# Out-projection by Strassen's seven products, with sums made beside the mixer, and the sums of w_ff1 on GpSimd in the first third of ff1

## The chip, the cores and the metric

The kernel runs on one core of one Trainium2 chip. The metric is the device time of one execution in microseconds. A core has five engines that run their own streams of instructions and wait for each other by semaphores: TensorE (PE, with its weight loads, PEld), VectorE (DVE), ScalarE (ACT), GpSimd (POOL) and SyncE (SP). In this kernel SP issues every DMA.

## What is computed

One layer of a streaming encoder. 2048 prompt rows and 128 rows of running streams make 17 chunks of 128 tokens; the model is 1024 wide. Cut to what matters here:

```python
proj = einsum('bld,de->ble', x, w_in)                  # in-projection
y_g = gmlp(proj)      # u * (W_s v + b), v normalised   (1024 wide)
y_s = ssd(proj)       # Mamba-2 scan, gated norm        (1024 wide)
h = einsum('ble,ed->bld', concatenate([y_g, y_s]), w_out)   # out-projection, 2048 -> 1024
x = layer_norm(ALPHA * x + h)
x = layer_norm(ALPHA * x + square(relu(x @ w_ff1)) @ w_ff2)  # 1024 -> 4096 -> 1024
```

## The kernel before

**Precision.** Every large matmul is made of three: both operands are split into a rounded high part and a rest (`split`: ScalarE casts, VectorE subtracts, L54 to L56), and high x high, high x low and low x high are summed in PSUM (`PASSES`).

**The mixer** (`mixer_heads`, L91) runs the in-projection in three blocks of 6, 6 and 5 chunks. A block has 18 units, each with one weight tile of 2 MB (`load_w`, L112) that is loaded one unit ahead into one of two buffers. The results u, v, z and xs go to DRAM. Between units, tasks of a list run, one per unit: `ssd` (chunk by chunk and by two groups) writes its rows to `ys_d`, `gmlp` (L511) reads v and u, makes the gate on TensorE (`sg`, L537), finishes it on VectorE (`og`, L545) and GpSimd (`ug`, L546), and writes `yg_d` (L547). yg is stored with features on the partitions, as the out-projection's matmuls need it, ys with tokens on the partitions; `load_blocks` and `flip` (L34 to L43) turn it in 32 x 32 squares by four DMAs and a VectorE transpose. The gMLP of the last block's five chunks (12 to 16) is left over when the in-projection ends; `mixer_heads` returns `run`, by which out_proj starts these tasks as `tail`.

**The out-projection** (`out_proj`, L617) holds all of w_out in SBUF, split, in eight tiles (`wout`, from loads `wos`). It goes chunk by chunk: 16 feature blocks, three passes and two halves of the output are 96 matmuls of 128x512 (L683). The first group has chunks 0 and 1, 192 matmuls, and `tail(1)` is called before each of its eight weight tiles. For each chunk `load_yg` and `load_ys` load and split the mix (`mx`); after the matmuls VectorE adds the residual (L708) and makes the LayerNorm (`layer_norm`, L604), and the row goes to `x1_d`. While this goes on, `during_out_proj` (L799) makes sums of w_ff1 (`w1_piece`, L771) on VectorE and stores them, and the first sums of x (`x_piece`).

**The FFN** (`ffn`, L815) already works by Strassen's seven products (Winograd's form) in 2 x 2 blocks: chunks are paired as in `THIRDS`, features halved. ff1 goes in thirds of the chunks, each over 16 groups g of w_ff1, loading the plain parts (`w1l`, `w1r`) and the stored sums (`w1s`). In thirds 2 and 3 `w2_piece` (L785) makes the sums of w_ff2 and stores them for ff2, which goes product by product.

**What sets the order.** The tile framework schedules the program ahead of time and fixes a stream for each engine; a tile that takes the place of another waits until that one's last reader is done. SP's stream is in order: a DMA that waits holds all those behind it. The DMAs share eight completion semaphores in turn.

## Time and profile before

| what | us |
|---|---|
| median of 3 runs (2840.2 to 2848.67) | 2842.54 |
| the profiled execution | 2838.33 |
| its span | 2836.5 |
| mixer: up to the first out-projection matmul | 0 to 1066.8 |
| out_proj, TensorE busy 386.49 of 1066 to 1471 | 1066.8 to 1471 |
| ff1, TensorE busy 677.84 of 1479 to 2174 | 1478.9 to 2174 |
| ff2 and the end, TensorE busy 647.91 of 2174 to 2836 | 2174 to 2836.5 |

The profile shows one execution. Section 1 of its page gives busy time by engine. A row of a group of instructions names line, engine, operation and tiles with their count, then busy time and the mean duration in ns, then the idle time of the engine ahead of them with what ended it. A row of a table by windows gives start and end, the length, the busy time of PE, PEld, DVE, ACT and POOL with their instructions, the granted TensorE clock, the DMA engines' busy share and GB/s. A row of the timeline gives start, duration, engine, line, operation and, in brackets, idle time before it with its releaser. A DMA row ends with KB of one and us from issue to landing.

### The profile page before, as it was taken

What the parts mean: (1) busy time and instruction counts of PE and PEld (TensorE: products, weight loads), DVE (VectorE), ACT (ScalarE), POOL (GpSimd) and SP (SyncE); (2) the same over time, 40 slices, a digit from 0 to 9 for tenths busy, and PEclk for the clock granted to TensorE, in tenths of its full rate; (3) what the DMA queues carried; (4) which work ended last, traced back from release to release, by engine and by line L of the source; (5) the groups of instructions that cost most, each with busy time, mean ns of one, the idle gap of its engine ahead of it and who ended that gap; (6) DMA issues with size and microseconds to landing.
All of it is one profiled execution on the core that took longest, in us unless ns stands there. A gap on an engine that the chain in (4) does not pass through costs nothing.

```text
span 2836.5 us, 42155 instructions
## 1 busy us (share of the span) xinstructions
PE 2755.8 (97%) x15814; PEld 2525.9 (89%) x15814; DVE 1811.7 (64%) x2852; ACT 1097.7 (39%) x2024; POOL 395.0 (14%) x547
## 2 busy tenths in 40 slices
...
GB/s 316 255 301 247 280 295 258 226 224 212 225 299 228 253 204 306 274 262 264 160 225 356 325 341 354 348 305 241 280 235 237 159 163 187 172 149 180 257 216 167
DMA packets 490012, 708.21 MB, mean 250 GB/s; under 512 B 74304, under 2 KB 378832, under 8 KB 483280
## 3 DMA queue, kind: packets, MB, share of 16 engines
...
HBM read 474.04 MB, written 231.39 MB: 249 GB/s over the span
## 4 chain that ended last, share of the span: by engine, by line
PE 76%; DMA 12%; DVE 7%; SPq 1%; issue 1%; ACT 1%; POOL 1%; ACTq 0%; DVEq 0%; POOLq 0%
PE pf L880 22%; PE pf L1068 21%; PE psfl L231 12%; PE pstl L239 10%; PE po L683 4%; PE yd L446 2%; DMA w1s<-w1p 2%; DMA w1p<-in_w_ff 2%; PE pf L1033 2%; DMA xv<-xtt 1%; PE sg L537 1%; PE st L483 1%; DMA e<-at 1%; DMA v<-vo 1%; PE yo L489 1%
## 5 line engine op out<-in xcount | busy, mean ns | idle before, releaser
L880 PE MATMUL pf<-xt,w 128*128 128x384 f32 (+1 forms) x4032 | 672.9, 329 | 24.7 <-ACT w L55 13.6
L880 PEld LDWEIGHTS pf<-xt,w 128*128 128x128 f32 x4032 | 669.5, 189 | 28.2 <-ACT w L55 14.4
L1068 PE MATMUL pf<-w,ht 128*128 128x512 f32 x2688 | 618.0, 389 | 0.7 <-ACT ht L55 0.7
L1068 PEld LDWEIGHTS pf<-w,ht 128*128 128x128 f32 x2688 | 504.4, 188 | 105.8 <-ACT ht L55 1.1
L231 PE MATMUL psfl<-xw,w 128*128 128x384 f32 (+1 forms) x2880 | 495.5, 330 | 0.1
L231 PEld LDWEIGHTS psfl<-xw,w 128*128 128x128 f32 x2880 | 475.9, 188 | 9.4 <-issue 9.0
L239 PE MATMUL pstl<-w,xw 128*128 128x256 f32 (+1 forms) x3264 | 410.2, 286 | 8.5 <-ACT w L55 6.6
L239 PEld LDWEIGHTS pstl<-w,xw 128*128 128x128 f32 x3264 | 395.6, 189 | 21.3 <-issue 12.0
L683 PE MATMUL po<-wout,mx 128*128 128x512 f32 x1632 | 378.9, 393 | 14.1 <-ACT mx L55 9.7
L683 PEld LDWEIGHTS po<-wout,mx 128*128 128x128 f32 x1632 | 308.2, 190 | 81.4 <-ACT mx L55 10.7
L56 DVE TENSOR_TENSOR ht<-hr,ht 128x1536 fp32r<-128x1536 f32 (+1 forms) x84 | 132.3, 1576 | 185.2 <-ACT ht L55 183.3
L55 ACT CAST ht<-hr 128x1536 fp32r<-128x1536 f32 (+1 forms) x84 | 112.3, 1337 | 214.8 <-PE pf L1068 192.7
L76 POOL TENSOR_SCALAR frs<-fmv 128x1 f32<-128x1 f32 x17 | 8.9, 525 | 1303.0 <-DVE fmv L987 1302.4
L56 DVE TENSOR_TENSOR w<-w2r,w 128x512 fp32r<-128x512 f32 x192 | 124.5, 684 | 61.1 <-ACT w L55 60.9
L55 ACT CAST w<-w2r 128x512 fp32r<-128x512 f32 x192 | 110.9, 618 | 135.5 <-PE pf L1068 93.4
L55 ACT CAST w<-w1s 128x512 fp32r<-128x512 f32 x192 | 118.1, 619 | 83.7 <-PE pf L880 74.3
L56 DVE TENSOR_TENSOR w<-w1s,w 128x512 fp32r<-128x512 f32 x192 | 131.3, 687 | 25.8 <-ACT w L55 19.9
L308 DVE SCALAR_TENSOR_TENSOR acc<-raw,cw,acc 128x640 f32<-128x640 f32 (+1 forms) x108 | 114.0, 1055 | 18.3 <-ACT acc L302 16.9
L438 ACT ACTIVATE e<-e,nacum 128x128 f32<-128x128 f32 x272 | 83.6, 389 | 71.9 <-POOL e L69 71.9
L247 ACT ACTIVATE gt<-gt 128x256 f32<-128x256 f32 (+1 forms) x116 | 52.3, 451 | 95.2 <-DVE gt L246 95.2
L871 ACT ACTIVATE hc<-hc 128x384 f32<-128x384 f32 (+3 forms) x144 | 87.1, 608 | 2.0
L55 ACT CAST mx<-mxs 128x512 fp32r<-128x512 f32 x34 | 20.1, 620 | 171.2 <-PE po L683 87.2
...
## 6 DMA issues: line engine op xcount, KB each, us to landing
...
w<-w_x SPq DMA_DIRECT2D x12, 2048.0 KB, 10.4
w1r<-in_w_ff SPq DMA_DIRECT2D x48, 512.0 KB, 7.9
...
w2r<-w2s SPq DMA_DIRECT2D x80, 256.0 KB, 4.6
ws<-in_w_in SPq DMA_DIRECT2D x34, 512.0 KB, 7.5
e<-at SPq DMA_DIRECT2D x34, 512.0 KB, 7.0
```

The costliest lines, as they stand in the source:

```text
L55: nc.scalar.copy(hi, src)
L56: nc.vector.tensor_sub(lo, src, hi.bitcast(F32))
L231: nc.tensor.matmul(ps[:, :n], w[:, a, k, f * P:(f + 1) * P], xw[:, b, k, o:o + n], start=(q, i, k) == KORDER[0], stop=(q, i, k) == KORDER[-1])
L239: nc.tensor.matmul(ps[:, :n], xw[:, a, k, j * P:(j + 1) * P], w[:, b, k, :n], start=(q, i, k) == KORDER[0], stop=(q, i, k) == KORDER[-1])
L308: nc.vector.scalar_tensor_tensor(aa, raw[:, k:k + npr], cw[:, ft, k:k + 1], aa, op0=ALU.mult, op1=ALU.add)
L438: nc.scalar.activation(e[:, h], e[:, h], AF.Exp, bias=s["nacum"][:, i:i + 1])
L446: nc.tensor.matmul(yd[:, h * HD:(h + 1) * HD], e[:, h], xdt[:, h * HD:(h + 1) * HD], start=True, stop=True)
L683: nc.tensor.matmul(acc[c][d], m[c][k // 4][:, a, k % 4], W[q][:, w, i, d * 512:(d + 1) * 512], start=k == 0 and (a, w) == (0, 0), stop=k = ...
L871: nc.scalar.activation(t, t, AF.Square)
L880: nc.tensor.matmul(o, W[i][:, u, k], X[i][:, v, k, :n], start=q + k == 0 and not more, stop=q == 2 and k == 3, skip_group_check=True)
L1033: nc.tensor.matmul(ps[d], h[:, u, k, f], w[d][:, v], start=k + f + q == 0, stop=(k, f, q) == (n - 1, 1, 2))
L1068: nc.tensor.matmul(acc[l], h[:, u, m, j * P:(j + 1) * P], w[m][:, v], start=kg + q + m == 0, stop=(kg, q, m) == (3, 2, 3))
```

## The change

The out-projection becomes Strassen's as well. Two chunks l and r are the row blocks of a 2 x 2 form, and the 2048 features and 1024 outputs are halved: the first half of the features is half of yg and half of ys. Eight pairs, (0,3), (1,4), (2,5), (6,9), (7,10), (8,11), (12,14) and (13,15), need seven products each, chunk 16 four plain ones (1, 2, 0, 3): 60 products of 24 matmuls of 128x512.

- The task `mix` replaces `gmlp`. After the gMLP of a pair's right chunk it makes the pair's sums: for yg (part 0) four loads of 256 KB, for ys (part 1) 16 loads of 64 KB and four transposes; four sums of 128x512 on VectorE in each part; 11 stores to `mv[p]`. That is 31 DMAs a pair. Sums, loads and the gMLP use one ring of eight tiles (`half`).
- w_out is no longer kept whole: `load_w(i)` loads the parts of one product's weights, subtracts on VectorE, and splits. A product's weights are loaded during the product before. `seq` gives the order: product 1 of all pairs and chunk 16, then 2, 0 (chunk 16 alone), 6, 7, 5, and 4 and 3 alternating.
- The partial results stay in SBUF (`y`, 17 tiles). The residual's additions (`add_x`) are made by GpSimd in product 5, and GpSimd multiplies and adds in the LayerNorm of the left chunks (`finish`); the right ones' is on VectorE.
- `tail(1)` is called ahead of the first five pairs of product 1, and the rest at the sixth.
- The first `x_piece` calls move behind product 3 of pairs 1 to 3.
- `w1_piece` goes. In ff1's first third GpSimd makes the sums of w_ff1, four operations of 128x512 for each g, and stores them; the other thirds load them.
- `w2_piece` goes. ff2's weight loads subtract on VectorE (32 operations of 128x1024), and product 4 runs ahead of 3. The residual there is added in halves between passes.

```diff
+THIRDS = [([0, 1, 2], [3, 4, 5]), ([6, 7, 8], [9, 10, 11]), ([12, 13], [14, 15])]
+ODD = 16
...
+    partner = {r: (k, l) for k, (l, r) in enumerate(p for t in THIRDS for p in zip(*t))}
+
+    def flipped(c, q):
+        s = half("fs").rearrange("p (a f) -> p a f", a=4)
+        for i in range(4):
+            nc.sync.dma_start(s[32 * i:32 * i + 32],
+                              ys_d[c][:, 256 * i + 128 * q:256 * i + 128 * q + 128].rearrange("(a j) f -> j a f", j=32))
+        t = half("ft").rearrange("p (k t) -> p k t", k=4)
+        flip(nc, t, s)
+        return t
+
+    def mix(b, j):
+        gmlp(b, j)
+        r = BLOCKS[b][0] + j
+        if r == ODD:
+            for q in range(2):
+                nc.sync.dma_start(mv[-1][:, 4, 4 * q:4 * q + 4], flipped(r, q))
+        if r not in partner:
+            return
+        p, l = partner[r]
+        for part in range(2):
+            tile4 = lambda name: half(name).rearrange("p (k t) -> p k t", k=4)
+            if part == 0:
+                a11, a12, a21, a22 = (tile4("ma") for i in range(4))
+                for t, c, q in ((a11, l, 0), (a12, l, 1), (a21, r, 0), (a22, r, 1)):
+                    nc.sync.dma_start(t, yg_d[c][:, 4 * q:4 * q + 4])
+            else:
+                a11, a12, a21, a22 = (flipped(c, q) for c in (l, r) for q in range(2))
+                nc.sync.dma_start(mv[p][:, 4, :4], a11)
+                nc.sync.dma_start(mv[p][:, 4, 4:], a12)
+                nc.sync.dma_start(mv[p][:, 5, 4:], a22)
+            to = lambda v: mv[p][:, v, 4 * part:4 * part + 4]
+            s1, s2, s3 = (tile4(f"ms{i}") for i in range(3))
+            nc.vector.tensor_add(s1, a21, a22)
+            nc.sync.dma_start(to(2), s1)
+            nc.vector.tensor_sub(s2, s1, a11)
+            nc.sync.dma_start(to(0), s2)
+            nc.vector.tensor_sub(s3, a11, a21)
+            nc.sync.dma_start(to(1), s3)
+            nc.vector.tensor_sub(s1, a12, s2)
+            nc.sync.dma_start(to(3), s1)
...
-            tasks += [(gmlp, b, j) for j in range(n)]
+            tasks += [(mix, b, j) for j in range(n)]
...
+    yl = pool("yl", 1)
+    wr = pool("owr", 4)
+    mp = pool("mo", 3)
+    mr = pool("mr", 2)
+    wq = pool("wq", 16)
...
+    b11, b12, b21, b22 = ((f, d) for f in range(2) for d in range(2))
+    PARTS = {1: (b11,), 2: (b21,), 3: (b22,), 6: (b11, b12, b22), 7: (b12, b22), 5: (1,), 4: (2, b21), 0: (b12,)}
...
+    def load_w(i):
+        out = []
+        for k in range(4):
+            s = None
+            for n, part in enumerate(PARTS[i]):
+                t = wr.tile([P, 2, 512], F32, name="wor", tag="wr")
+                load_part(t, part, k)
+                if n:
+                    nc.vector.tensor_sub(t, t, s)
+                if n and i == 6:
+                    nc.sync.dma_start(made[k][n - 1], t)
+                s = t
+            for m in range(2):
+                w = wq.tile([P, 2, 512], F32R, name="wo", tag="w")
+                split(w[:, 0], w[:, 1], s[:, m])
+                out.append(w)
+        return out
+
+    V = {6: 0, 7: 1, 5: 2, 3: 3}
+
+    def load_mix(i, p):
+        s = mr.tile([P, KD, P], F32, name="mxs", tag="mr")
+        if p < len(pairs) and i in V:
+            nc.sync.dma_start(s, mv[p][:, V[i]])
+        else:
+
+            c = ODD if p == len(pairs) else pairs[p][i == 4]
+            k = slice(0, 4) if i in (0, 1) else slice(4, 8)
+            nc.sync.dma_start(s[:, :4], yg_d[c][:, k])
+            nc.sync.dma_start(s[:, 4:], mv[p][:, 5 if i == 4 else 4, k])
+        t = mp.tile([P, 2, KD, P], F32R, name="mx", tag="mx")
+        split(t[:, 0], t[:, 1], s)
+        return t
+
...
+    def add_x(c, x, d):
+        h = slice(512 * d, 512 * d + 512)
+        nc.gpsimd.tensor_add(y[c][:, h], y[c][:, h], x[:, h])
...
+        eng.tensor_mul(y[c], y[c], g1)
+        eng.tensor_add(y[c], y[c], b1)
+        nc.sync.dma_start(x1_d[c], y[c])
...
+        if i == 5:
+            nc.vector.tensor_add(yd, yc, ps)
+            nc.vector.tensor_add(yb, yb, ps)
+            x = scaled(l)
+            add_x(l, x, 0)
+            add_x(l, x, 1)
+            x = scaled(r)
+            add_x(r, x, 0)
+            add_x(r, x, 1)
+        if i == 4:
+            stat(r, 1)
+            stat(l, 0)
+            nc.vector.tensor_add(yc, yc, ps)
+            finish(r, (0,), nc.vector)
+        if i == 3:
+            nc.vector.tensor_add(yb, yb, ps)
+            finish(l, (1,), nc.gpsimd)
+
+    n = len(pairs)
+    seq = [(i, p) for i in (1, 2) for p in range(n + 1)] + [(0, n)] + [(i, p) for i in (6, 7, 5) for p in range(n)]
+    seq += [(4, 0)] + [s for p in range(n - 1) for s in ((4, p + 1), (3, p))] + [(3, n - 1), (3, n)]
...
+        nx = order.index(i) + 1
+        if nx < len(order) and order[nx] not in W and (p == 0 or i == 0):
+            W[order[nx]] = load_w(order[nx])
+        if k + 1 < len(seq):
+            ahead[seq[k + 1]] = load_mix(*seq[k + 1])
+        mx = ahead.pop((i, p))
+        at += 1
+        if i == 1 and p < 5:
+            tail(1)
+        acc = pss[at % len(pss)].tile([P, 512], F32, name="po", tag="a")
+        for q, (u, v) in enumerate(PASSES):
+            for m in range(KD):
+                nc.tensor.matmul(acc, mx[:, u, m], W[i][m][:, v], start=q + m == 0, stop=(q, m) == (2, KD - 1))
+        if (i, p) == (1, 5):
             tail(NCH)
             right.close()
...
+            g1 = cp.tile([P, D], F32, name="g1")
+            nc.sync.dma_start(g1, A["ln1_g"].unsqueeze(0).to_broadcast([P, D]))
+            b1 = cp.tile([P, D], F32, name="b1")
+            nc.sync.dma_start(b1, A["ln1_b"].unsqueeze(0).to_broadcast([P, D]))
+        evict(i, p, acc)
+        if i == 3 and 1 <= p <= 3:
+            sums.x_piece(0, p - 1)
...
-    def w1_piece(self, g, ring):
...
-    def w2_piece(self, g):
...
-        w = wr.tile([P, 4, P], F32, name="w1l", tag="wr")
-        nc.sync.dma_start(w, A["w_ff1"][g][:, :4, :P])
+        w = wr.tile([P, 4, 2, P], F32, name="w1l", tag="wr")
+        if b == 0:
+            nc.sync.dma_start(w.rearrange("p k f n -> p k (f n)"), A["w_ff1"][g][:, :4])
+        else:
+            nc.sync.dma_start(w[:, :, 0], A["w_ff1"][g][:, :4, :P])
         v = wr.tile([P, 4, 2, P], F32, name="w1r", tag="wr")
         nc.sync.dma_start(v.rearrange("p k f n -> p k (f n)"), A["w_ff1"][g][:, 4:])
         s = sump.tile([P, 2, 4, 2, P], F32, name="w1s", tag="ws")
-        nc.sync.dma_start(s.rearrange("p h k f n -> p h (k f n)"), sums.w1[g])
-        return {1: w, 2: v[:, :, 0], 4: v[:, :, 1], 6: s[:, 0, :, 0], 7: s[:, 0, :, 1], 3: s[:, 1, :, 0], 5: s[:, 1, :, 1]}
+        flat = s.rearrange("p h k f n -> p h (k f n)")
+        a11, a21, a12, a22 = (t[:, :, f] for t in (w, v) for f in range(2))
+        s2, s3, s4, s1 = (s[:, h, :, f] for h in range(2) for f in range(2))
+        if b == 0:
+            nc.gpsimd.tensor_add(s1, a21, a22)
+            nc.gpsimd.tensor_sub(s2, s1, a11)
+            nc.gpsimd.tensor_sub(s3, a11, a21)
+            nc.gpsimd.tensor_sub(s4, a12, s2)
+            nc.sync.dma_start(sums.w1[g], flat)
+        else:
+            nc.sync.dma_start(flat, sums.w1[g])
...
-        if b > 0 and g % 2:
-            sums.w2_piece(8 * (b - 1) + g // 2)
...
+    t1, t2 = (lambda g: [made[g][0]]), (lambda g: [made[g][1]])
+    PARTS = {1: (b11,), 2: (b21,), 3: (b22,), 6: (b11, b12, b22), 7: (b12, b22), 5: (t1,), 4: (b21, t2)}
...
+                if n:
+                    nc.vector.tensor_sub(t, t, s)
+                    if i == 6:
+                        nc.sync.dma_start(made[g][n - 1], t)
...
-    runs = [(i, (0, 1, 2)) for i in (1, 2, 6, 7, 5, 3)] + [(4, (0, 1)), (4, (2,))]
+    runs = [(i, (0, 1, 2)) for i in (1, 2, 6, 7, 5, 4)] + [(3, (0, 1)), (3, (2,))]```

The order in which the instructions stand shows what becomes of the seam between mixer and out-projection. First SyncE's queue at the mixer's end. The program before: `w_v` is a weight tile of the last units, `v<-vo` are stores of the last units' results, `ys` are SSD rows, `wos` are parts of w_out.

```order
L117 DMA w<-w_v_3834 128x16x256 [waits DMAHW7_49,PE_49]
L631 DMA wos<-in_w_out 128x1024 [waits DMAHW0_49,DVE_49]
L266 DMA v_8147<-vo 128x5x256 [waits DMAHW1_49,DVE_49]
L523 DMA v<-v_8147 128x512 [waits DMAHW3_49,DMAHW2_49,DMAHW1_49]
L525 DMA ug<-u_8146 128x4x128
L631 DMA wos<-in_w_out 128x1024 [waits DMAHW4_49,DMAHW0_49,DVE_49]
L266 DMA v_8147<-vo 128x5x256 [waits DMAHW5_49,DVE_49]
L631 DMA wos<-in_w_out 128x1024 [waits DMAHW6_49,DMAHW4_49,DVE_49]
```

The changed program at the same place: `g` and `b` are ln1's rows, `wor` are parts of product 1's weights, `mxs` is the mix of the first pair.

```order
L839 DMA g_12563<-in_ln_g 128x1024 [waits DMAHW4_49,PE_49]
L511 DMA ys_109<-xs 128x512 [waits DMAHW5_49,DVE_49]
L841 DMA b_12565<-in_ln_b 128x1024 [waits DMAHW6_49]
L269 DMA v_8339<-vo 128x5x256 [waits DMAHW7_49,DVE_49]
L687 DMA wor<-in_w_out 128x2x512 [waits DMAHW3_49]
L687 DMA wor<-in_w_out 128x2x512 [waits DMAHW1_49]
L687 DMA wor<-in_w_out 128x2x512 [waits DMAHW2_49,Activation_49]
L687 DMA wor<-in_w_out 128x2x512
L550 DMA yg_88<-ug 128x512 [waits DMAHW4_49,Pool_49]
L721 DMA mxs<-yg_76 128x512 [waits DMAHW5_49]
L722 DMA mxs<-mv_127 128x512 [waits DMAHW6_49]
```

Before, parts of w_out stand between the last units' stores. Now product 1's weights stand behind g's load, whose semaphore from PE is reached by the last matmul of the in-projection (the tile takes the place of the mixer's `xw`).

Second, TensorE's stream around the leftover gMLPs. The program before: `sg` is half a gMLP, `po` the out-projection.

```order
L537 MATMUL sg<-wt,v 128x128 x4
L683 MATMUL po<-wout,mx 128x512 x79
L537 MATMUL sg<-wt,v 128x128 x4
L683 MATMUL po<-wout,mx 128x512 x5
L537 MATMUL sg<-wt,v 128x128 x4
L683 MATMUL po<-wout,mx 128x512
L537 MATMUL sg<-wt,v 128x128 x4
L683 MATMUL po<-wout,mx 128x512 x11
L537 MATMUL sg<-wt,v 128x128 x8
L683 MATMUL po<-wout,mx 128x512 x24
```

The changed program, from the two halves of chunk 14's gMLP on:

```order
L540 MATMUL sg<-wt,v 128x128 x4
L829 MATMUL po<-wo,mx 128x512 x32
L540 MATMUL sg<-wt,v 128x128 x4
L829 MATMUL po<-wo,mx 128x512 x64
L540 MATMUL sg<-wt,v 128x128 x8
L829 MATMUL po<-wo,mx 128x512 x24
L540 MATMUL sg<-wt,v 128x128 x8
L829 MATMUL po<-wo,mx 128x512 x1272
```

The first x8 is chunk 15's gMLP, the x24 behind it product 1 of the pair 13/15, and the last x8 chunk 16's. Six products of other pairs stand ahead of chunk 15's.

Third, SyncE's queue further on, where chunk 15's v is loaded (`L526`, as `L523` before). The program before, with loads of w_out and of w_ff1's pieces between the gMLPs:

```order
L547 DMA yg_90<-ug 128x512
L631 DMA wos<-in_w_out 128x1024
L547 DMA yg_90<-ug 128x512
L525 DMA ug<-u_8146 128x4x128
L631 DMA wos<-in_w_out 128x1024
L523 DMA v<-v_8147 128x512
L783 DMA w1s_11521<-w1p 128x1024
```

The changed program: `fs` are quarters of the SSD rows of chunks 12 and 14, `ft` their transposes, `ms` sums, `mv_133` the stored mix of the pair 12/14.

```order
L564 DMA fs<-ys_105 32x4x128 x5
L587 DMA mv_133<-ft 128x512
L564 DMA fs<-ys_107 32x4x128 x4
L588 DMA mv_133<-ft 128x512
L722 DMA mxs<-mv_133 128x512
L564 DMA fs<-ys_107 32x4x128 x4
L589 DMA mv_133<-ft 128x512
L593 DMA mv_133<-ms_12255 128x512
L526 DMA v<-v_8339 128x512
L595 DMA mv_133<-ms_12256 128x512
```

The load of chunk 15's v now stands behind the sums of the pair 12/14 and their stores.

262 lines of the change are left out of this document (118 added, 144 removed).

## The prediction

> **What bounds the kernel now.** I read the page's busy shares first, then one table of busy time by windows, then TensorE's timeline around the start of out_proj.
>
> ```profile
> span 2836.5 us, 42155 instructions
> PE 2755.8 (97%) x15814; PEld 2525.9 (89%) x15814; DVE 1811.7 (64%) x2852; ACT 1097.7 (39%) x2024; POOL 395.0 (14%) x547
> L683 PE MATMUL po<-wout,mx 128*128 128x512 f32 x1632 | 378.9, 393 | 14.1 <-ACT mx L55 9.7
> ```
>
> TensorE is busy for 97% of the span, so a matmul that goes is worth its time, provided that nothing new makes TensorE wait. Only some 80 us of the span are TensorE idle; the change must not add to them. The windows' columns are length, then busy time of PE, weight loads, DVE, ACT, POOL, then granted clock, DMA share and GB/s.
>
> ```profile
> 400.00:800.00 400.00, 395.16 (x2713) 382.11 (x2712) 236.46 (x429) 129.69 (x319) 119.82 (x146) 0.99 0.73 236
> 1060.00:1100.00 40.00, 34.44 (x189) 29.20 (x188) 30.91 (x63) 12.08 (x21) 10.82 (x15) 0.96 0.87 275
> 1100.00:1140.00 40.00, 36.22 (x161) 28.93 (x160) 29.91 (x47) 10.34 (x11) 10.00 (x6) 0.92 0.95 324
> 1160.00:1200.00 40.00, 40.00 (x178) 33.12 (x177) 19.50 (x27) 4.98 (x8) 4.20 (x4) 1.00 0.79 244
> 1480.00:1520.00 40.00, 30.61 (x145) 28.50 (x144) 35.28 (x49) 20.88 (x33) 2.87 (x4) 0.84 1.05 380
> 1520.00:1720.00 200.00, 200.00 (x1155) 200.00 (x1154) 152.90 (x267) 111.44 (x194) 0.00 (x0) 1.00 0.98 337
> 2400.00:2836.50 436.50, 421.91 (x1861) 348.69 (x1859) 273.49 (x336) 157.69 (x195) 32.82 (x51) 0.99 0.58 191
> ```
>
> In 1160 to 1200 out_proj alone runs without a gap: 40.00/178 = 0.2247 us a matmul. The seam where the mixer ends (1060 to 1140) costs 5.56 + 3.78 = 9.3 us of TensorE idle, though five chunks of gMLP still run there: the out-projection's first two chunks fill the waits.
>
> ```profile
> 1065.01 1.05 PE L537 MATMUL sg<-wt,v 128*128 128x128 f32 x8
> 1066.82 1.19 PE L683 MATMUL po<-wout,mx 128*128 128x512 f32 x4 [0.76 <-ACT mx L55]
> 1125.74 74.43 PE L683 MATMUL po<-wout,mx 128*128 128x512 f32 x327 [1.55 <-DVE wout L637]
> ```
>
> Out_proj's first matmul stands 0.76 us after the mixer's last; its weights were already in SBUF.
>
> **1. Matmuls.** 17 x 16 x 3 x 2 = 1632 become 60 products of 24 = 1440. 192 x 0.2247 = **-43 us**. (The group's busy time gives 378.9/1632 = 0.232 us, so 45; its mean of 393 ns counts the overlap of neighbours and isn't used.) TensorE bounds this stage, so the saving stands wherever the matmuls run without gaps.
>
> **2. The seam.** This is the largest term. Three things change there. In the new order g1's load waits for the mixer's last matmul, and the queue SP is in order: the weights of product 1 and its first mixes stand behind it. Call that matmul's end T0. Second, products need whole pairs: pairs 12/14 and 13/15 exist only when mix has read both chunks' gMLP and SSD rows back from DRAM, added, and stored. So "with the mixer" holds for six pairs; the sums of the last two are made inside out_proj, on TensorE's path. Third, product 1 has one matmul step per pair (24 x 0.2247 = 5.4 us), not 192 matmuls, to put between two gMLPs.
>
> ```profile
> DMA packets 12462, 20.58 MB, mean 322 GB/s; under 512 B 937, under 2 KB 7252, under 8 KB 12459
> yg<-ug SPq DMA_DIRECT2D x10, 256.0 KB, 6.3
> v<-v SPq DMA_DIRECT2D x9, 256.0 KB, 6.4
> ```
>
> ```profile
> mxs<-yg SPq DMA_DIRECT2D x2, 512.0 KB, 3.4
> mys<-ys SPq DMA_DIRECT2D x8, 128.0 KB, 2.8
> ```
>
> ```profile
> L37 SPq DMA_DIRECT2D mys<-ys x68: 302/427/1153, 1072.0 to 1411.4; - x68
> DMA to landing us min/median/max: 2.0/4.1/10.0
> ```
>
> ```profile
> L546 POOL TENSOR_TENSOR ug<-ug,og x34: 1268/1672/2202, 393.1 to 1124.6; 128x512 f32<-128x512 f32 x34
> DMA to landing us min/median/max: 3.2/5.2/9.1
> ```
>
> ```profile
> L545 DVE SCALAR_TENSOR_TENSOR og<-sg,lgh,cst 128x128 f32<-128x128 f32 x136 | 38.0, 340 | 10.6 <-PE sg L537 10.6
> L778 DVE TENSOR_TENSOR w1p<-w1p 128x512 f32<-128x512 f32 x16 | 11.0, 689 | 60.7 <-DMA w1p<-in_w_ff 55.4 <-issue 5.3
> L43 DVE STREAM_TRANSPOSE myt<-mys 128x1024 f32<-128x1024 f32 x17 | 21.1, 1243 | 16.5 <-DMA mys<-ys 16.3
> L55 ACT CAST mx<-mxs 128x512 fp32r<-128x512 f32 x34 | 20.1, 620 | 171.2 <-PE po L683 87.2 <-DMA mxs<-yg 79.2 <-DVE x L612 4.8
> ```
>
> These are the seam's DMAs (1066 to 1130), the same kinds in a quiet stretch (1375 to 1440), issue and landing of ys and yg, and the arithmetic of a hop.
>
> - Start: g1, b1, one v, four weight parts and the first mix are 4.8 MB; at 322 GB/s, 15 us idle before the first product.
> - Six steps (6 x 5.4) and six half gMLPs (6 x 1.06) then run to T0 + 54, where TensorE comes to chunk 15's gMLP. Its v load stands on SP behind all of mix(12,14). Counted in the new order, 50 DMAs with 17 MB stand from T0 to that mix's last yg load, 12 of them weight parts of 0.5 MB (6.3 MB), among them four of product 6, which are wanted 90 us later: 17/322 = T0 + 53. Then, one after another on SP: landing 3.4; four sums 4 x 0.69 = 2.8; three times four ys loads, a half transpose and the store that waits for it (1.7 + 2.8 + 0.6 = 5.1 each); the load of the stored mix, which waits for that store, 2.0; two sums 1.4; v's landing 3.4. That is 28, so v comes at T0 + 80 and TensorE idles 26.
> - From chunk 15's gMLP to product 1 of pair 13/15: four og 1.4, two GpSimd multiplications 3.3, store 3.4, loads 3.4, sums 2.8, two rounds of ys 10.2, store 2.0, mix load 3.4, cast and subtraction 1.3: 31, of which 30 idle.
> - Chunk 16's rows, with product 1 of 13/15 running beside, 7.
>
> 15 + 26 + 30 + 7 = 78; less the 9 of before, **+69**. With every landing at ys's least, 2.0, and the 380 GB/s of 1480 to 1520, the parts are 13, 15, 23 and 0: +41. With landings at the medians of the busy seam (4.1 to 6.4): 15, 38, 40, 10: +94. I take the quiet stretch's landings, as SP itself waits in most of these hops and so little else flies.
>
> The Trainium skill, DMA: Bandwidth & Descriptors, section "Anatomy of one DMA", gives a DMA about 2.0 us fixed plus its bytes at 436 GB/s, fitted on another issuing path; as an estimate a 256 KB load is then 2.6 us, and the term would be near +46. The trace's yg row, 3.2 at the least, stands above it.
>
> **3. Products 5, 4, 3.** GpSimd now makes the residual's additions (32 of 128x512) and half the LayerNorm's multiplications and additions (16 of 128x1024, each like two).
>
> ```profile
> L76 POOL TENSOR_SCALAR lrs<-lmv 128x1 f32<-128x1 f32 x17 | 16.9, 994 | 330.0 <-DVE lmv L609 330.0
> L77 POOL TENSOR_TENSOR lrs<-lrs,mhalf 128x1 f32<-128x1 f32 x17 | 13.1, 768 | 1.4
> L991 POOL TENSOR_SCALAR fnm<-fmv,frs 128x1 f32<-128x1 f32 x17 | 12.4, 734 | 1.6
> ```
>
> (32 + 32) x 1.67 = 107, and 17 x (0.99 + 0.77 + 0.73) = 42: 149 us of GpSimd against 25 steps x 5.4 = 135 of TensorE, and ff1's first rows wait for the last LayerNorms. **+12**, 0 to 30.
>
> **4. The mixer's blocks.** Each pair adds 31 DMAs, 31 x 0.43 = 13 us of SP, and up to 14 of them stand between two weight loads.
>
> ```profile
> w<-w_u SPq DMA_DIRECT2D x4, 2048.0 KB, 9.0
> ```
>
> A unit lasts 1066/54 = 20 us, the load 9.0 of them, 14 issues 6: about 5 us are left for waits within a mix, and a mix has several. DVE's additional 48 us (8 pairs x 8 sums x 0.69, and half transposes) and 38 MB lie under the matmuls (59% and 73% in 400 to 800). **+8**, 0 to 30.
>
> **5. ff1 and ff2.** 64 GpSimd sums x 1.67 = 107 us within a third of ff1's 695 (1479 to 2174), 232, ahead of splits on DVE, 76% busy (1520 to 1720): **+2**, 0 to 15. ff1's start, 9.4 us idle in 1480 to 1520 before, may win those or lose as many: 0. The w_ff1 pieces' 64 DVE operations in out_proj and their 32 MB were under matmuls: nothing. The w_ff2 sums move from ff1 to ff2, where DVE is 63% busy: nothing; without that cover 32 x 1.25 = 40.
>
> Sum: -43 + 69 + 12 + 8 + 2 = **+48**. The profiled run took 2838.33 us for its span of 2836.5, 0.15% under the median of 2842.54, so I put the sum on the median: **2890 us**. A measurement of this kernel tells about 0.3%, 8.5 us, from no change.
>
> **The rivals.**
> - A, faster: the seam stays covered, since v arrives when TensorE comes for it. For it: five gMLPs cost 9.3 us before with loads of 6.4. Against it: there nothing was read back and added in between. It decides if chunk 15's v lands by T0 + 54. Then -43, with terms 3 to 5 between 0 and 22: 2800 to 2821, say **2811**. Chance 0.18.
> - B, the seam at its lower bound: -43 + 41 + half of 22 = +9, **2851**. For it: in the quiet stretch landings were already at 2.8, near that least. Against it: the seam's own medians are twice as long. 0.14.
> - D, slower: the mixer's weight loads fall behind on SP. From 5 us of waits a mix the next unit starts late; ten boundaries with 6 us more: +60 in place of +8, **2942**. For it: each sum's store waits for DVE on SP. Against: two weight buffers. 0.12.
> - E, slower: GpSimd and DVE take turns.
>
> ```profile
> L501 DVE TENSOR_TENSOR xs<-xs,yt x32: 635/1100/1551, 190.3 to 1027.4; 128x512 f32<-128x512 f32 x32
> L56 DVE TENSOR_TENSOR wout<-wos,wout 128x1024 fp32r<-128x1024 f32 x8 | 9.7, 1220 | 9.7 <-ACT wout L55 9.7
> ```
>
> One addition of the same shape takes 0.64 to 1.55 us in the mixer, where GpSimd works too. If they exclude each other, products 5 to 3 need GpSimd 64 x 1.27 + 42 = 123 and DVE's two-input SBUF operations, 25 mixes and 18 of r's LayerNorm x 1.22 + 16 weights x 0.7 = 64: 187 against 135 is +52, 40 more than term 3: **2930**. 0.10. The Trainium skill, SBUF — State Buffer, section "Who interferes with whom", states such an exclusive lock against GpSimd; L501's spread agrees with it, while a mixer that is 99% TensorE shows it can be harmless.
>
> **How the numbers follow.** The forecast has 0.46, around it the terms' bounds taken as independent give 2858 to 2935. The range 2815 to 2940 takes in B, E, half of A and half of D, and leaves out some 0.15 to 0.2. Faster: A's 0.16 and 0.04 of B, 0.20. Same: 0.02 of A, 0.05 of B, 0.03 of the forecast, 0.10. Slower: the rest, 0.70.
>
> **What would show it.** Right: out_proj's first product starts some 15 us after the mixer's last matmul; TensorE's timeline shows two gaps of over 20 us, before chunk 15's sg (released by DVE's v, behind it SP) and before product 1 of pair 13/15 (by ACT's mx); then steps of 5.4 us without gaps until product 5. Wrong: gaps in product 1 of under 30 us together (A), weight waits at unit boundaries in the mixer above 20 us (D), L501-like rows growing in products 5 to 3 with mx released late (E).

## The result, and the profile after

The changed kernel takes 2953.72 us (2951.94 to 2962.46), the one before 2841.37: 1.0395 of it, 95% interval 1.0366 to 1.0424. It is slower, as forecast, but by 112 us where 48 were forecast, and lies outside the range. The profiled execution has a span of 2952.2 against 2836.5, 115.7 more.

The page's first lines and the groups of the in-projection, the out-projection and ff1:

```profile
span 2952.2 us, 42598 instructions
PE 2746.5 (93%) x15622; PEld 2514.5 (85%) x15622; DVE 1932.6 (65%) x2917; ACT 1199.7 (41%) x2148; POOL 584.2 (20%) x678
...
L968 PE MATMUL pf<-xt,w 128*128 128x384 f32 (+1 forms) x4032 | 678.6, 330 | 45.3 <-ACT xt L57 41.4
...
L234 PE MATMUL psfl<-xw,w 128*128 128x384 f32 (+1 forms) x2880 | 494.4, 331 | 19.7 <-DMA w<-w_u 14.3
...
L829 PE MATMUL po<-wo,mx 128*128 128x512 f32 x1440 | 345.2, 402 | 68.8 <-ACT mx L57 60.6
```

TensorE's idle time is now 206 us (2952.2 - 2746.5) where it was 81 (2836.5 - 2755.8). Most of the difference stands in three places: in the mixer, two thirds of it in front of weights; in front of out_proj's mixes and gMLPs; and in front of ff1's X.

The same division of the span in both kernels by windows: the mixer (two rows), out_proj, the start of ff1, the rest. Before:

```profile
0.00:520.00 520.00, 501.22 (x3296) 477.98 (x3297) 343.86 (x602) 213.83 (x461) 152.35 (x244) 0.99 0.86 277
520.00:1066.80 546.80, 541.95 (x3904) 520.59 (x3902) 324.95 (x559) 186.47 (x484) 161.23 (x204) 1.00 0.72 232
1066.80:1471.40 404.60, 386.79 (x1704) 317.57 (x1704) 243.85 (x353) 56.30 (x82) 45.70 (x44) 0.98 0.78 245
```

After, with out_proj in three rows (seam, middle, products 5 to 3):

```profile
0.00:520.00 520.00, 497.00 (x3243) 474.37 (x3244) 344.06 (x599) 212.99 (x460) 142.81 (x235) 0.98 0.87 279
520.00:1117.40 597.40, 563.40 (x3957) 535.86 (x3955) 352.59 (x628) 185.19 (x483) 170.71 (x213) 0.98 0.80 257
1117.40:1244.30 126.90, 62.05 (x264) 50.86 (x264) 57.70 (x107) 29.29 (x46) 17.61 (x15) 0.72 0.75 250
1244.30:1450.00 205.70, 196.32 (x856) 161.78 (x857) 124.37 (x142) 89.05 (x119) 40.50 (x27) 0.98 0.71 234
1450.00:1562.00 112.00, 96.49 (x394) 76.25 (x392) 97.84 (x110) 37.97 (x39) 67.81 (x61) 0.95 0.69 215
1562.00:1635.00 73.00, 28.95 (x121) 26.80 (x122) 52.64 (x53) 27.92 (x36) 36.17 (x29) 0.67 0.96 317
```

- **Mixer**: 1066.8 to 1117.4, **+50.6**. TensorE idle there 1117.4 - 497.0 - 563.4 = 57.0 against 23.6: +33.4. Of its waits 22.5 are for weight loads that land late (19.7 in the group of L234, 2.8 at L242), where before there was 0.1; those for a gMLP's v rose from 1.0 to 8.4. The other 17.2 are busy time for the same matmuls, beside a lower granted clock (0.98 in these two rows, 0.99 and 1.00 before).
- **Out_proj**: 404.6 to 444.6, **+40.0**. Busy 386.8 to 354.9: -31.9 where 192 matmuls at full clock are -43, so 11 went to slower matmuls (clock 0.72 in the seam). Idle 17.8 to 89.7: +71.9, 64.9 of it in the seam.
- **From out_proj's last matmul to ff1's first**: 7.5 to 32.5, **+25.0**. From there to the end: 1357.6 and 1357.7.

TensorE's timeline of the seam and of ff1's start:

```profile
1116.35 1.05 PE L540 MATMUL sg<-wt,v 128*128 128x128 f32 x8
1136.35 7.15 PE L829 MATMUL po<-wo,mx 128*128 128x512 f32 x24 [18.95 <-ACT mx L57]
...
1160.49 14.79 PE L829 MATMUL po<-wo,mx 128*128 128x512 f32 x64
1193.06 2.08 PE L540 MATMUL sg<-wt,v 128*128 128x128 f32 x8 [17.79 <-DVE v L529]
1196.86 2.08 PE L540 MATMUL sg<-wt,v 128*128 128x128 f32 x8 [1.73 <-DVE v L529]
1222.60 8.29 PE L829 MATMUL po<-wo,mx 128*128 128x512 f32 x24 [23.66 <-ACT mx L57]
```

```profile
1594.52 1.65 PE L968 MATMUL pf<-xt,w 128*128 128x384 f32 x4 [32.53 <-ACT xt L57]
```

What X waits for in those 32.5 us is this:

```profile
1580.51 2.34 POOL L755 TENSOR_TENSOR y<-y,b 128x1024 f32<-128x1024 f32 x1
1582.87 0.33 SPq L756 DMA_DIRECT2D x<-y  x1
1585.55 0.91 SPq L916 DMA_DIRECT2D xr<-xv  x2
```

GpSimd's last LayerNorm addition of a left chunk ends at 1582.85, its row is stored, and X's first load (`xr`) is issued 2.7 us behind that store.

The seam is as foretold: 19 us before the first product, 18 before chunk 15's gate, 24 before product 1 of its pair. What the forecast did not have are the size of the mixer's loss and ff1's start. In the mixer a weight load is late because of what stands ahead of it on SP. Its queue before the 5.9 us wait at 611 to 617:

```profile
599.50 0.34 SPq L587 DMA_DIRECT2D mv<-ft  x1
599.93 0.38 SPq L426 DMA_DIRECT2D bc<-bc  x1
600.37 1.96 SPq L564 DMA_DIRECT2D fs<-ys  x4
602.42 0.38 SPq L588 DMA_DIRECT2D mv<-ft  x1
602.90 0.38 SPq L428 DMA_DIRECT2D e<-at  x1
603.32 1.87 SPq L564 DMA_DIRECT2D fs<-ys  x4
605.23 0.43 SPq L282 DMA_DIRECT2D z<-zo  x1
605.76 0.54 SPq L120 DMA_DIRECT2D w<-w_u  x1
```

Eight loads and two stores of a mix and three other DMAs go ahead of the 2 MB of `w<-w_u` in these 6 us, and each store waits for a transpose. The unit whose buffer these weights take had ended at 594.5, so the load goes out 11 us late; the weights then need 11 us more.

### The profile page after: what moved, and what is told of

Read it like the earlier page. It is cut to its first block, busy times and chain, and to the rows that moved or that the text cites. A ratio compares the mean times of both kernels' runs of the same rounds, so it can differ in the third digit from the quotient of the medians.

```text
span 2952.2 us, 42598 instructions
## 1 busy us (share of the span) xinstructions
PE 2746.5 (93%) x15622; PEld 2514.5 (85%) x15622; DVE 1932.6 (65%) x2917; ACT 1199.7 (41%) x2148; POOL 584.2 (20%) x678
## 4 chain that ended last, share of the span: by engine, by line
PE 65%; DMA 15%; DVE 8%; POOL 3%; SPq 3%; issue 3%; ACT 2%; DVEq 0%; ACTq 0%; POOLq 0%
PE pf L1185 21%; PE pf L968 19%; PE psfl L234 9%; PE pstl L242 7%; PE po L829 4%; PE yd L449 2%; DMA xts<-x 2%; PE pf L1150 1%; DMA wor<-in_w_out 1%; DMA e<-at 1%; DMA fs<-ys 1%; DMA w<-w_z 1%; DMA mv<-ms 1%; SPq L564 1%; DMA v<-v 1%
## 5 line engine op out<-in xcount | busy, mean ns | idle before, releaser
L968 PE MATMUL pf<-xt,w 128*128 128x384 f32 (+1 forms) x4032 | 678.6, 330 | 45.3 <-ACT xt L57 41.4
L968 PEld LDWEIGHTS pf<-xt,w 128*128 128x128 f32 x4032 | 675.0, 189 | 49.0 <-ACT xt L57 43.5
L234 PE MATMUL psfl<-xw,w 128*128 128x384 f32 (+1 forms) x2880 | 494.4, 331 | 19.7 <-DMA w<-w_u 14.3
L234 PEld LDWEIGHTS psfl<-xw,w 128*128 128x128 f32 x2880 | 479.6, 190 | 24.0 <-issue 23.5
L242 PE MATMUL pstl<-w,xw 128*128 128x256 f32 (+1 forms) x3264 | 412.6, 286 | 12.0 <-ACT w L57 6.8
L242 PEld LDWEIGHTS pstl<-w,xw 128*128 128x128 f32 x3264 | 399.2, 191 | 21.8 <-issue 8.7
L829 PE MATMUL po<-wo,mx 128*128 128x512 f32 x1440 | 345.2, 402 | 68.8 <-ACT mx L57 60.6
L829 PEld LDWEIGHTS po<-wo,mx 128*128 128x128 f32 x1440 | 278.6, 195 | 133.2 <-ACT mx L57 63.7
L58 DVE TENSOR_TENSOR ht<-hr,ht 128x1536 fp32r<-128x1536 f32 (+1 forms) x84 | 132.3, 1578 | 128.0 <-ACT ht L57 125.9
L57 ACT CAST ht<-hr 128x1536 fp32r<-128x1536 f32 (+1 forms) x84 | 112.2, 1337 | 194.4 <-PE pf L1185 152.5
L58 DVE TENSOR_TENSOR w<-w1s,w 128x512 fp32r<-128x512 f32 x192 | 143.0, 748 | 34.2 <-ACT w L57 30.6
L57 ACT CAST w<-w1s 128x512 fp32r<-128x512 f32 x192 | 117.9, 616 | 51.5 <-PE pf L968 41.5
L57 ACT CAST w<-w2r 128x512 fp32r<-128x512 f32 x144 | 83.1, 618 | 86.9 <-PE pf L1185 57.8
L58 DVE TENSOR_TENSOR w<-w2r,w 128x512 fp32r<-128x512 f32 x144 | 93.8, 687 | 35.3 <-ACT w L57 34.8
L57 ACT CAST mx<-mxs 128x1024 fp32r<-128x1024 f32 x60 | 62.5, 1045 | 130.5 <-DMA mxs<-mv 76.9
L441 ACT ACTIVATE e<-e,nacum 128x128 f32<-128x128 f32 x272 | 83.6, 389 | 78.6 <-POOL e L71 78.5
L58 DVE TENSOR_TENSOR mx<-mxs,mx 128x1024 fp32r<-128x1024 f32 x60 | 85.8, 1430 | 25.1 <-ACT mx L57 24.5
L57 ACT CAST w<-w1r 128x512 fp32r<-128x512 f32 x96 | 59.4, 618 | 89.8 <-PE pf L968 89.8
```

The source lines that it names most:

```text
L57: nc.scalar.copy(hi, src)
L58: nc.vector.tensor_sub(lo, src, hi.bitcast(F32))
L234: nc.tensor.matmul(ps[:, :n], w[:, a, k, f * P:(f + 1) * P], xw[:, b, k, o:o + n], start=(q, i, k) == KORDER[0], stop=(q, i, k) == KORDER[-1])
L242: nc.tensor.matmul(ps[:, :n], xw[:, a, k, j * P:(j + 1) * P], w[:, b, k, :n], start=(q, i, k) == KORDER[0], stop=(q, i, k) == KORDER[-1])
L441: nc.scalar.activation(e[:, h], e[:, h], AF.Exp, bias=s["nacum"][:, i:i + 1])
L829: nc.tensor.matmul(acc, mx[:, u, m], W[i][m][:, v], start=q + m == 0, stop=(q, m) == (2, KD - 1))
```

## The experiments

Durations of M (mixer, up to the wait before out_proj's first matmul) and O (from there to out_proj's last matmul) are read from each trace as above. The kernels of 2 to 4, 6 to 8 and 13 leave some or all of the sums out of the result and measure time alone.

**1. The FFN's changes alone** (`e1_ffn_only`): mixer and out_proj of before, without `w1_piece`, with the changed FFN.

```diff
-        for g in range(NG * n // 13, min(NG * (n + 1) // 13, NG)):
-            self.w1_piece(g, ring)
         if n in (4, 6, 8):
             self.x_piece(0, n // 2 - 2)
```

> The mixer and the out-projection of before (without the w_ff1 pieces on VectorE) with the FFN of the changed kernel: sums of w_ff1 on GpSimd in the first third, sums of w_ff2 in ff2. My theory: these two moves are hidden, since the changed kernel's ff1 and ff2 together last as long as before (1357.7 us from ff1's first matmul to the end, against 1357.6). So 2842 us, within 8. Rival: GpSimd's sums cost time in the first third, or the out-projection gains where 64 VectorE operations and 32 MB go: then outside 2834 to 2850.

Measured: 2819.76, ratio 0.9929 (0.9905 to 0.9954). **Faster than both kernels**, 0.7% under the one before; the rival holds. From ff1's first matmul on it takes as long as before (1357.6); the gain is in out_proj:

```profile
1071.80:1455.10 383.30, 381.00 (x1704) 315.21 (x1704) 204.16 (x289) 57.13 (x82) 46.14 (x44) 1.00 0.58 171
```

Without 64 VectorE sums and 32 MB, TensorE is idle for 2.3 us of out_proj, where it was 17.8, and the clock is 1.00. My "were under matmuls: nothing" was wrong by 21 us (404.6 to 383.3), of which 5 are lost again ahead of out_proj's first matmul (1071.8 for 1066.8). "The w_ff2 sums move from ff1 to ff2 [...]: nothing" and the first third's GpSimd sums (+2) held, taken together.

**2. No mixes** (`e2_no_mix`).

```diff
-            tasks += [(mix, b, j) for j in range(n)]
+            tasks += [(gmlp, b, j) for j in range(n)]
...
+        nc.sync.dma_start(s[:, :4], yg_d[c][:, 4:])
+        nc.sync.dma_start(s[:, 4:], yg_d[c][:, :4])
```

> The changed kernel without the pairs' sums: the task is the gMLP alone, and each product loads plain yg rows in place of stored sums (which leaves the sums out of the computation). My theory: all of the mixer's 51 us and the two waits of 18 and 24 us at its seam come from the mixes. Then the mixer ends at 1066 within 8, the seam keeps the wait of 19 us before the first product, and the whole takes 2853, within 15 (2954 less 51, less some 50 of waits and slow clock). Rival: the mixer is long for another reason (more memory for other pools, other order of the SSD tasks): it ends after 1100, and the whole stays above 2890.

Measured: 2839.25, one run, as expected. M is 1068.8, O 378.1: the mixes cost 115 us, 48.6 in the mixer and 66.5 in out_proj. Even with free sums this kernel gains nothing on the one before, and is slower than experiment 1: against that one's O, which is 385.9 with the 2.5 us of wait ahead of it, the 192 matmuls leave 8, and ff1 waits 29.2 in place of 8.1.

**3 and 4. Mixes whose stores wait for no sum** (`e3_free_stores`: a constant tile; `e7_og_stores`: the gate tile that the gMLP has just finished).

```diff
-            nc.sync.dma_start(to(2), s1)
+            nc.sync.dma_start(to(2), wt[:, :4])     # e3; kept[0] in e7
```

> The changed kernel with all of the mix's 31 DMAs a pair, its VectorE sums and its transposes, but each of its 11 stores writes a constant tile that was loaded long before, so that no store waits for VectorE (which leaves the sums out of the result). My theory, that weight loads come late because SP stands in stores that wait: the mixer ends at 1075, within 10, and the whole takes 2890 within 20. Rival, that the DMAs' number and their 38 MB make the weight loads late by themselves: the mixer ends at 1105 or later, as in the changed kernel (1117).

> As the kernel with constant stores, but each store of a mix writes the gate tile of the gMLP just ahead of it (og), which is done by then, so that the stores keep their place in time and still wait for no sum and no transpose (which leaves the sums out of the result). My theory: the mixer ends at 1080, within 10. Rival, bytes and number of DMAs: 1105 or later.

Measured: 2931.38 and 2927.26, one run each. The first can't be read: with nothing to wait for, the scheduler put stores into the first 150 us, where two new waits of 11.1 and 24.4 us stand (M 1117.2, O 418.0). In the second the last in-projection matmul ends at 1080, as I expected, but the SSD's last tasks then come behind it, in the open, and M is 1120.9:

```profile
915.51 16.65 PE L242 MATMUL pstl<-w,xw 128*128 128x256 f32 x120 [11.61 <-DMA w<-w_z]
...
1078.88 1.43 PE L242 MATMUL pstl<-w,xw 128*128 128x256 f32 x10
1086.26 3.67 PE L449 MATMUL yd<-xdt,e 128*128 128x64 f32 x16 [5.96 <-ACT e L441]
...
1099.54 3.67 PE L449 MATMUL yd<-xdt,e 128*128 128x64 f32 x16 [5.65 <-POOL xdt L444]
...
1127.91 6.62 PE L832 MATMUL po<-wo,mx 128*128 128x512 f32 x18 [7.00 <-ACT wo L57]
```

So "the mixer's end" by its last in-projection matmul was the wrong thing to forecast. M isn't the same work here either: five more half gMLPs stand ahead of the first product (240 matmuls `sg` for 200). By the end of the last SSD task and in-projection matmul the mixer gains 10 us (1106.7 for 1116.5), by the start of the first product 8; the other 20 are gained from there to out_proj's end. The first row shows that weights can be late though no store of a mix waits for a sum: from 891 to 905 SP issues 19 other DMAs ahead of that load, eleven of them a mix's stores.

**5. The stores on ScalarE's queue** (`e6_act_stores`).

```diff
-            nc.sync.dma_start(to(2), s1)
+            nc.scalar.dma_start(to(2), s1)
```

> The changed kernel with the mix's 11 stores a pair issued by ScalarE, all else the same. My theory, that the weight loads are late because SP stands in these stores: the waits for w in the mixer (5.9, 4.9, 8.1 us) go and the mixer ends near 1085, within 12; the whole 2920, within 15. Rival 1: the waits are for the loads that stand ahead of a mix's weight load (20 loads and their landings), or bytes: the mixer ends at 1110 or later. Rival 2: ScalarE then stands in the stores and holds the activations: waits for ACT take the place of those for w.

Measured: 2955.44, ratio 1.0402 (1.0378 to 1.0427), no gain. The waits for weights shrink from 22.5 us to 9.7 in all, the longest from 8.1 to 3.3, and the in-projection ends at 1084. The SSD tasks behind it take all of it back: waits for their `xdt` rise from 7.2 to 26.2 us.

```profile
1089.69 3.67 PE L449 MATMUL yd<-xdt,e 128*128 128x64 f32 x16 [5.99 <-POOL xdt L444]
...
1106.64 3.68 PE L449 MATMUL yd<-xdt,e 128*128 128x64 f32 x16 [9.33 <-POOL xdt L444]
...
1152.48 7.71 PE L829 MATMUL po<-wo,mx 128*128 128x512 f32 x20 [6.89 <-ACT wo L57]
```

My theory that SP's stores alone make the mixer late falls: the waits for weights were one face of it, the late SSD tasks are another. Their loads stand on SP too: the rows of the last task are loaded at 1124.54, behind the store of the task before at 1122.52, and its `xdt` starts at 1127.22. Why the scheduler leaves four of these tasks behind the in-projection here, and two in experiment 4, isn't shown.

**6 to 8. Parts of a mix**: the yg half alone (`e11_yg_only`), the ys half alone (`e12_ys_only`), loads and sums without stores (`e17_no_stores`).

```diff
-        for part in range(2):
+        for part in range(1):       # e11; (1,) in e12
...
-            nc.sync.dma_start(to(2), s1)      # e17: all 11
```

> The changed kernel with the mix's yg half alone: four loads, four sums, four stores a pair in place of 31 DMAs; in place of the ys half each product loads plain yg rows (which leaves the ys half out of the computation). My theory, that a mix costs by the DMAs and round trips that it puts on SP: 23 of 31 DMAs and three of the four round trips are gone, so most of the 115 us between the changed kernel (2954) and the one without mixes (2839) comes back: 2870, within 15. Rival, that the cost is the yg half, which reads rows back that the gMLP has only just stored: above 2910.

> The counterpart: the mix's ys half alone, 16 loads of 64 KB, four transposes, four sums and seven stores a pair; the yg half of each product is loaded as plain rows (which leaves the yg sums out). My theory: 2925, within 15. Rival (the yg half is the cost): below 2890.

> The changed kernel with the mix's 20 loads, sums and transposes a pair, but without its 11 stores; products load plain rows (which leaves the sums out of the result). If the stores cost by their waits alone, this equals the kernel whose stores wait for nothing: 2927 within 10. If the loads and their landings make the mixer late, it stays above 2915. If the stores cost by number and bytes, it comes near the kernel without mixes: 2870 or less.

| kernel | DMAs a pair | M | O | whole |
|---|---|---|---|---|
| no mixes | 0 | 1068.8 | 378.1 | 2839.25 |
| yg half | 8 | 1071.3 | 398.6 | 2866.06 |
| no stores | 20 | 1082.0 | 416.3 | 2895.6 |
| ys half | 23 | 1089.4 | 417.5 | 2903.43 |
| stores that wait for no sum (e7) | 31 | 1120.9 | 412.5 | 2927.26 |
| stores on ScalarE's queue (e6) | 20 on SP, 11 on ScalarE | 1145.6 | 415.9 | 2955.44 |
| the changed kernel | 31 | 1117.4 | 444.6 | 2953.72 |

Each row but the last two is one run. The yg half came out as expected (2866 for 2870); the ys half costs 64 us where I said 86, and the two halves together 24 more than their sum, 27 + 64. The kernel without stores lies between its three forecasts (2870, 2915, 2927) and settles none.

The mixer's loss grows with the number of a pair's DMAs: 2.5, 13, 21 and 49 us for 8, 20, 23 and 31. It does so where no store waits, too (no stores, and e7). But the bytes and VectorE's work grow with the number, and these runs don't tell the three apart; nor does the number on SP alone give the order, since e6, with 20 there, is the latest of all. TensorE waits for a weight load only in the kernels with 31 DMAs (22.5 us in the changed one, 13.6 in e7, 9.7 in e6). With 8 to 23 it never does, and the loss stands in waits for the tasks' v and xdt and in slower matmuls. Differences of a few us in M tell nothing: the changed kernel and those of 9 to 12 and 14, whose mixer is the same, have M from 1109.1 to 1119.1. In out_proj the stores' waits matter more: from the first product to its end it takes 425.7 us, and 405.5 in e7.

**9. Product 2 of six pairs into the seam** (`e5_seam`).

```diff
-    seq = [(i, p) for i in (1, 2) for p in range(n + 1)] + [(0, n)] + ...
+    seq = [(i, p) for a in (range(6), range(6, n + 1)) for i in (1, 2) for p in a]
+    seq += [(6, 0), (6, 1), (6, 2), (0, n)] + [(6, p) for p in range(3, n)] + ...
```

> The changed kernel with product 2 of the first six pairs ahead of product 1 of the last two pairs and chunk 16 (same 60 products, weights in two sets of eight tiles, chunk 16's product 0 moved into product 6). My theory: in the changed kernel TensorE waits 17.8 and 23.7 us in the seam because only six steps of 5.4 us stand ahead of chunk 15's gMLP and of the pair 13/15; eight steps now stand ahead of the gMLP and four more ahead of the pair, so these two waits fall to under 15 together, and the slow clock behind them goes: 2915, within 15. Rival: the weights of products 2 and 6, loaded earlier, push the v loads and the mixes back on SP by as much as TensorE gains: above 2940.

Measured: 2956.14, ratio 1.0409 (1.0379 to 1.0438). My theory falls, the rival holds:

```profile
1204.29 2.07 PE L540 MATMUL sg<-wt,v 128*128 128x128 f32 x8 [19.42 <-DVE v L529]
1209.58 2.08 PE L540 MATMUL sg<-wt,v 128*128 128x128 f32 x8 [3.21 <-DVE v L529]
1239.07 2.08 PE L540 MATMUL sg<-wt,v 128*128 128x128 f32 x8 [27.42 <-DVE v L529]
```

Two more products stand ahead of chunk 15's gate, but its v comes 93.8 us after the mixer's last matmul (1204.29 - 1110.5) where it was 76.7 (1193.06 - 1116.35), behind product 2's weights, and chunk 16's, behind the second mix, is now waited for. So the products that were moved to fill the seam brought their own loads onto the queue that makes it long.

**10 to 12. The end of out_proj**: the left chunks' LayerNorm on VectorE (`e4_ln_dve`), the pools' order (`e10_pools`), both (`e14_pools_ln`).

```diff
-            finish(l, (1,), nc.gpsimd)
+            finish(l, (1,), nc.vector)      # e4, e14
...
-    yl = pool("yl", 1)
     wr = pool("owr", 4)
...
     wq = pool("wq", 16)
+    yl = pool("yl", 1)                      # e10, e14
```

> The changed kernel with the LayerNorm's multiplication and addition of the left chunks on VectorE, as the right ones'. My theory: the wait of 32.5 us before ff1's first matmul is the chain of the last LayerNorms on GpSimd, store, load, with X's first load behind the store on SP; with two operations of 1.2 in place of 2.3 and 2.3 and no GpSimd sum between them, it shrinks to 22 to 27, and the whole to 2940 to 2947. Rival: the wait is made by x's sums and the loads of their rows, which stay: 2954 within 4.

> The changed kernel with one line moved: the pool of the left chunks' rows (y) is opened last in out_proj, so that ff1's X tiles no longer take its place; in the new order X's first load stands ahead of the last rows' stores, where it stood behind chunk 13's. My theory: the wait of 32.5 us before ff1's first matmul is X's load, held on SP behind that store; it falls to 15 to 22, where the sums of w_ff1 for the first group on GpSimd and their splits end, and the whole to 2940, within 7. Rival: the first weights are as late as X (split at 1590 to 1596, X at 1597): the wait stays above 28 and the whole within 5 of 2954.

> The changed kernel, mixes and all, with both repairs. In the one with the pools alone the waits at ff1's start were 17 and 17 us, for the split of weights that stand behind GpSimd's LayerNorms and sums. My theory: without the LayerNorms GpSimd is free by then, and the 18 us that VectorE's LayerNorm gained ahead of out_proj's last matmul are kept: 2924, within 8. Rival: GpSimd's chain for chunk 16 and the first group's sums stay: above 2935.

Measured: 2950.61 (1.0387, 1.0358 to 1.0417), 2943.51 (1.0364, 1.034 to 1.0388) and 2936.47 (1.0333, 1.0315 to 1.0351). With VectorE, O falls by 18 (1540.7 - 1114.4 = 426.3), nearly all of it in products 5 to 3, which shows the price of GpSimd there: 93.7 us for 112.0, TensorE idle 3.8 for 15.5.

```profile
1447.00:1540.70 93.70, 89.87 (x385) 72.80 (x383) 84.25 (x108) 36.96 (x39) 34.62 (x46) 0.98 0.69 218
```

But ff1 then waits 8 longer, where I had expected 6 to 10 less, and the whole lies within the rival's 4 us of 2954:

```profile
1581.25 5.44 PE L968 MATMUL pf<-xt,w 128*128 128x384 f32 x16 [40.59 <-ACT xt L57]
```

X's load still stood behind the last rows' stores. With the pools alone (2940 was expected) the wait for X is gone and one for the weights appears, in two pieces:

```profile
1574.51 3.96 PE L968 MATMUL pf<-xt,w 128*128 128x384 f32 x12 [17.06 <-ACT w L57]
1595.21 5.11 PE L968 MATMUL pf<-xt,w 128*128 128x384 f32 x19 [16.74 <-ACT w L57]
```

That confirms why the wait was there (memory: X's tiles took the place of rows that were not yet stored) and that removing it uncovers the next one. In the profiled execution the first wait is 15.5 us shorter, and what follows ff1's first matmul is 10.2 longer; the mixer, which the edit doesn't touch, is 8.3 shorter. With both edits I expected 2924, and the rival, above 2935, holds: ff1 still waits 14.6 and 18.4 for weights.

**13. Both repairs without mixes** (`e13_bound`): the kernel of 2 with the edits of 10 and 11.

> The kernel without mixes (sums left out, plain rows loaded), with two repairs at ff1's start: the left chunks' rows in the last pool, so that X's loads don't stand behind their stores, and the left chunks' LayerNorm on VectorE. It bounds what the seven products could give if their sums were free. My theory: the wait of 29 us before ff1's first matmul falls to about 10, 2815 within 8, no faster than the kernel with the FFN's changes alone (2820). Rival: the start of ff1 is bound by the GpSimd sums for the first group: 2830 or more.

Measured: 2803.05, ratio 0.9875 (0.9855 to 0.9895), 12 less than expected. O is 351.2, 35 less than in experiment 1; ff1's start still waits 13.5 and 18.8. So seven products could pay, if their sums cost less than some 17 us (2819.76 - 2803.05); they cost 115, the yg half alone 27.

**14 and 15. The first group's sums of w_ff1 on VectorE** (`e15_first_dve` on 12, `e16_ffn_first_dve` on 1).

```diff
+            eng = nc.vector if g == 0 else nc.gpsimd
-            nc.gpsimd.tensor_add(s1, a21, a22)
+            eng.tensor_add(s1, a21, a22)
```

> The changed kernel with both repairs, and the four sums of w_ff1's first group on VectorE instead of GpSimd. My theory: the second wait at ff1's start (18.4 us) is GpSimd's chain, three LayerNorm scalars of chunk 16 and five sums that take 2.2 to 2.8 us each while VectorE works too; it falls under 6, the whole to 2921, within 7. Rival: X's loads, which stand behind the rows' stores on SP, are as late; the wait stays above 12 and the whole above 2930.

> The kernel with the FFN's changes alone (2820), and the first group's sums on VectorE. Its waits in ff1's first 40 us are 21 us in all, 8 of them ahead of the first matmul. My theory: some 5 of them are GpSimd's sums: 2815, within 5. Rival: it stays at 2820 within 3, since there GpSimd has no LayerNorm to multiply.

Measured: 2928.73 (1.0306, 1.0286 to 1.0325) and 2826.84 (0.9941, 0.9926 to 0.9956). In the first of the two the second wait falls from 18.4 to 15.0 only, where under 6 was expected, since VectorE's order puts those sums behind the last LayerNorms and the splits of X. VectorE there:

```profile
1573.18 1.22 DVE L755 TENSOR_TENSOR y<-y,b 128x1024 f32<-128x1024 f32 x1
1574.32 1.75 DVE L58 TENSOR_TENSOR xt<-xr,xt 128x1536 fp32r<-128x1536 f32 x1
1577.31 1.76 DVE L58 TENSOR_TENSOR xt<-xr,xt 128x1536 fp32r<-128x1536 f32 x1 [1.24 <-ACT xt L57]
1579.03 1.25 DVE L45 STREAM_TRANSPOSE xtt<-xts 128x1024 f32<-128x1024 f32 x1
1580.19 0.65 DVE L936 TENSOR_TENSOR w1s<-w1l,w1r 128x512 f32<-128x512 f32 x1
```

GpSimd's chain was not the cause of that wait by itself. On experiment 1 the edit gains nothing: 2826.84 is above both what I expected (2815) and its rival (2820), though the ratios' intervals overlap, and ff1's first 40 us have 23.5 us of waits for 21.0. The fastest complete kernel stays experiment 1.

## Why the prediction was wrong

| term | forecast | measured |
|---|---|---|
| 192 matmuls | -43 | -32, slower matmuls take 11 |
| seam | +69 | +56 (64.9 - 9.3), slower matmuls apart |
| products 5, 4, 3 and the middle of out_proj | +12 | +16 (71.9 - 56) |
| mixer | +8 | **+50.6** |
| ff1's start | 0 | **+25.0** |
| ff1's first third, rest | +2 | 0 |
| sum | +48 | +115.7 of the span |

The mechanism of the seam was right, waits, places and releasers. Term 3 was near in size (15.5 us idle in products 5 to 3), and experiment 10 shows it as GpSimd's, but not by the mechanism forecast, that GpSimd's 149 us outlast TensorE's 135: GpSimd is busy for 67.8 of 112 us there. What TensorE waits for is `mx`, and VectorE's split of it lengthens beside GpSimd's additions:

```profile
1537.75 3.09 POOL L754 TENSOR_TENSOR y<-y,g 128x1024 f32<-128x1024 f32 x1 [2.03 <-ACT y L753]
1538.49 3.43 DVE L58 TENSOR_TENSOR mx<-mxs,mx 128x1024 fp32r<-128x1024 f32 x1
1541.98 7.54 PE L829 MATMUL po<-wo,mx 128*128 128x512 f32 x32 [1.39 <-DVE mx L58]
```

The split takes 1.73 us in the mean from 1400 to 1562, 1.25 from 1250 to 1400, and 1.35 from 1400 on in experiment 10. That is rival E's sign, at far less than E's price (+52). Two steps failed.

**Term 4.** I wrote "about 5 us are left for waits within a mix, and a mix has several", and took 8 us for the mixer all the same. That was rival D: by its +60 in place of +8 the sum is 2942, and the measured 2954 is nearest to it. It had 0.12, and the range's upper end cut it in half. Its mechanism was half right. Weight loads are late: 22.5 us of waits, past the 20 that the prediction gave as D's sign; they are two thirds of the mixer's 33 us of added idle time. Yet taking the stores off SP shortened these waits and not the mixer: the SSD's loads share the queue, and their tasks came late in their place. I had counted the in-projection's matmuls as the mixer, not the tasks that have to be done by its end. I also left out the clock: beside the 33 us of idle time the mixer's matmuls took 17 more, at a lower granted clock.

**ff1's start.** "May win those or lose as many: 0". Term 3 named the wait ("ff1's first rows wait for the last LayerNorms") but had no price of its own for it. The new order, which I had, puts X's first load behind chunk 13's store, which waits for GpSimd's LayerNorm; a price could have been read from the rows: five GpSimd operations, a store, a load and a cast.

Beside these, "the w_ff1 pieces' 64 DVE operations and 32 MB were under matmuls: nothing" missed a gain of 21 us in out_proj. If the changed kernel has that gain too, the loss without it would be larger still; no run shows it by itself there. That VectorE was 60% busy there hid that TensorE waited 17.8 us.

On the rivals: A (2811) fell with the seam's waits; B's lower bound of the seam (+41) was passed; E's lengthened operations are in the rows above, but no run tried them by themselves.

Three sums of the prediction don't come out as written. The 48 us of VectorE are six pairs' sums and transposes, not eight's, which are 64 (from the kernel without mixes to the changed one VectorE's busy time in the mixer rose by 33). And the terms' bounds taken as independent reach up to some 2930, not 2935. The seam's estimate of +46 with loads of 2.6 us comes out only with the lower bound's 380 GB/s and nothing for chunk 16; with the landings alone changed, the same steps add up to some +64. The landing row of yg, 3.2 at the least, mixes its 256 KB stores with loads of 512 KB. None of this changes the forecast.

The Trainium skill, TensorE: Matmul & The Clock Gate, section "Part 1: The HAM clock gate", has the clock at half after an idle window of about 3.4 us. The rows agree in kind: the granted clock is 0.72 in the seam and 0.67 at ff1's start, and 0.98 in a mixer with 57 us of scattered waits.
